# Attention values split into high and low parts at eviction, stored by head, with read-backs of outputs issued ahead of the last store

## Chip, core and metric

The kernel runs on one NeuronCore of a Trainium2 chip. The metric is the device time of one execution in microseconds (us). The core has a matrix engine (TensorE, PE in the profile, with PEld for its weight loads), VectorE (DVE), ScalarE (ACT), GpSimd (POOL), and SyncE (SP), whose queue issues most DMAs; ACT has a DMA queue too. All DMAs run on the same 16 DMA engines.

## What is computed

One layer of a transformer encoder for 1024 positions of 1024 features, all in float32: an adaLN modulation computed from `c`, two attention branches side by side, a gated merge, and a ConvFFN. Cut to what matters here:

```python
h = rmsnorm(x, g_mix) * (1 + scale1) + shift1
qa, ka, va, qb, kb, vb, ga, gb = split(h @ w_in)     # 8 heads of 64 columns in each branch
oa = mixture_of_dilations(qa, ka, va, rel_bias)      # windows (128,1), (512,4), (2048,16), merged per position
ob = neighbourhood_attention_2d(qb, kb, vb, na_rpb)  # 16 x 64 grid, 8 rows x 16 columns around each query
merged = sigmoid(ga) * (oa @ w_branch_dil) + sigmoid(gb) * (ob @ w_branch_na)
x = x + gate1 * (merged @ w_out)
h2 = rmsnorm(x, g_ffn) * (1 + scale2) + shift2
u_val, u_gate = split(depthwise_conv_seq(h2 @ w_up))
x = x + gate2 * ((gelu(u_gate) * u_val) @ w_down)
return rmsnorm(x, g_final)
```

## The kernel before, in words

**Precision.** A float32 operand is split into a rounded high part and a remainder, both of a type that TensorE multiplies at full rate (`FR`). A product is then three matmuls, high by high, high by low, low by high. The split is one ACT copy (`hi`) and one subtraction (`lo`) on DVE or POOL.

**Order of work.** Inside `tc.manual_schedule` (line 524 and 1356 to 1359) each engine executes its instructions in the order in which the program writes them; outside, a planner orders them. A tile of a pool with `bufs=n` reuses its buffer after n others, and the engine that writes it anew waits for its last reader, a DMA included.

**Projection (about 50 to 142 us).** `v_product`, `v_parts` and `v_wide` compute the values of both branches. A block is 128 positions (`st`, 0 to 7). Branch A's blocks 0 to 3 come in two halves of 256 columns; blocks 4 to 7 and all eight of branch B in one tile of 512 columns (`v_wide`). The order is `v_steps` (line 651): A's blocks 4 and 5 together in the two banks `pj` of `ps_g`, then 6 and 7 in the three banks `pv` of `ps_s`, then a step `None`, then B's blocks 0 to 7 in `pv`. Step `None` splits B's value weights (`v_split`: ACT the high parts, DVE and POOL the low ones), multiplies Q and K of the second position half in the two `pj` banks (lines 733 to 738), and starts POOL on sums for the next stage (`t_sums`) and on `a_operands`, which has one DVE subtraction (line 460) behind POOL's work.

In each step the program writes the matmuls, then `row_pairs` (a few multiply-adds of DVE over tiles of `w_ada`, 512 KB each, which SP loads seven ahead as their buffers come free, line 675), then `v_out` for the tiles of the step. `v_out` (line 313) copies the tile out of PSUM on ACT into one of two buffers `vs` and stores it: on SP's queue for the halves of blocks 0 to 3 and the last two blocks, on ACT's queue for the others. Values go to `va_s` or `vb_c` with one row of 512 columns per position.

**Rearranging in DRAM.** Keys' values are needed in chunks. `va_chunks` (line 412, six DMAs in step `None`) and `vb_chunks` (line 419, four calls of four DMAs in slots 54, 56, 59 and 61) copy the values from DRAM to DRAM into the order in which the heads read them.

**Heads (about 285 to 637 us).** Work is placed by hand in slots 0 to 101 (`at(slot, phase, job)`). A slot emits its jobs, phase by phase, and between them steps of `fill_steps`, matmuls of the gate columns of `w_in` that keep PE busy. `DilHead` (eight heads, one every 8 slots) and `NaHead` (eight heads, one every 4 slots from slot 64) load queries and keys, biases and values, multiply scores, apply softmax, turn the probabilities and multiply them by the values. `aside` queues ACT and DVE jobs to be emitted between fill steps, and `ensure(mark)` emits up to a mark.

The values of a head are loaded as float32 into the second half of a tile `vv` (`v_raw`, two buffers), three slots ahead of a `DilHead` (four DMAs) and two slots behind the start of a `NaHead` (four DMAs). `v_tile` (line 775) then splits them: ACT copies the high part to the first half, POOL subtracts in place.

`DilPair` merges the near and far outputs of two heads by shares: `send`, `load` of shares into two buffers `fb`, `weigh` on POOL in slots s0 + 27, 28, 30 and 31, `merge` in s0 + 32. Outputs go to `o_scr` in DRAM. `later(n, job)` puts a store n slots on; past the last slot it issues it at once.

**Hand-over (about 640 to 680 us).** Outputs are read back (`o_split`: a load into one of six buffers `oraw`, an ACT copy, a DVE subtraction), the gates are loaded (`gate_load`) and the branch weights `w_br` are loaded and split, all in `openers`, one at a fill step, while the last fill steps run. Then the branch products start.

Of the kernel before, what the change touches and what calls it, by code (L numbers as in the profile page):

```python
# [29 lines left out]
def hybrid_encoder(tc, xT, c, w_ada, small, w_in, p1_bias, p23_bias, na_bias, ln2_mult, ident, w_br, w_out,  # L30
# [8 lines left out]
    def f(ap):  # L39
        return ap.bitcast(FT)  # L40
# [239 lines left out]
    vb_c = dram.tile([S, 512], FT, name="vbc")  # L280
# [4 lines left out]
    v_scr = dram.tile([S + 9 * 128, 512], FT, name="v")  # L285
    va_s, va_b = v_scr[:S], v_scr[S:].rearrange("(j p) n -> j p n", j=9)
    vb_s = [v_scr[64 * sum(NA_NC[:cb]):64 * sum(NA_NC[:cb + 1])] for cb in range(4)]
# [24 lines left out]

    def v_out(br, st, p, c0=0, queue=sp):
        vs = work.tile([128, 512], FT, name="vs", bufs=2)[:, :p.shape[-1]]
        act.activation(vs, p, AF.Copy)
        queue.dma_start((va_s, vb_c)[br][st * 128:st * 128 + 128, c0:c0 + p.shape[-1]], vs)
# [94 lines left out]

    def va_chunks(cc):
        v4 = va_s.rearrange("(r t) n -> r t n", r=4)[:, :, cc]
        for r in range(4):
            sp.dma_start(va_b[1:8, 32 * r:32 * r + 32, cc], v4[r, 16:240].rearrange("(j p) n -> j p n", p=32))
        for j, t0 in ((0, 0), (8, 240)):
            sp.dma_start(va_b[j, 0:64, cc].rearrange("(r p) n -> r p n", r=4), v4[:, t0:t0 + 16])

    def vb_chunks(cb):
        t0, n = NA_T0[cb], NA_NC[cb]  # L420
        for r in range(4):
            sp.dma_start(vb_s[cb].rearrange("(w t r) n -> r w t n", r=4, t=n)[r],
                         vb_c[256 * r:256 * r + 256].rearrange("(w t) n -> w t n", t=16)[:, t0:t0 + n])
# [100 lines left out]
    with tc.manual_schedule(engines={e.engine for e in (sp, act, dve, pool, pe)}):  # L524
# [152 lines left out]
        def va_load(head, vr):  # L677
            cc = slice(64 * head, 64 * head + 64)
            sp.dma_start(vr[:, 0:8], va_s.rearrange("(t p) n -> p t n", p=128)[:, :, cc])
            sp.dma_start(vr[:, 8:15], va_b[1:8].rearrange("j p n -> p j n")[:, :, cc])  # L680
            for x_, j in ((0, 0), (64, 8)):
                sp.dma_start(vr[x_:x_ + 64, 15], va_b[j, 0:64, cc])

        def v_raw(load, head):
            vv = sm_pool.tile([128, 16, 128], FR, name="vv", bufs=2)
            load(head, f(vv[:, :, 64:128]))
            return vv
# [99 lines left out]
    for br, st in v_steps[10:]:  # L787
        v_out(br, st, *v_wide(st))
# [1310 lines left out]
```

## Time and profile before

| | |
|---|---|
| median of 3 runs | 1504.47 us (1503.78 to 1504.56) |
| profiled execution | 1502.23 us, of it the span of the instructions 1500.1 us |
| mean granted TensorE clock | 0.992 |
| TensorE busy | 97% of the span |
| DMA traffic | 241.13 MB, mean 161 GB/s |

The profile is of one execution. Its page gives busy times, the span in slices, the DMA queues, the chain of work that ended last, and the costliest groups. Answers of the trace show more: windows (busy time of each engine in a stretch, granted clock, share of the DMA engines in use), waits (who waited for whom), and the timeline (start, duration, engine, line, operation, what it writes and reads; in brackets the idle time ahead of it and what ended that). A row with "q" behind the engine's name (SPq, ACTq) is the issue of a DMA, not its transfer. Where an instruction waited for several things, the one that came last by the profile is named, which can be wrong where that engine had been done for long.

### The profile page before, as it was taken

Reading aid. Unit: us, or ns where it says so; the run is one execution under the profiler, and the core shown is the slowest. Engines: PE = TensorE matmul, PEld = TensorE weight load, DVE = VectorE, ACT = ScalarE, POOL = GpSimd, SP = SyncE. Lnnn points to the kernel's source line nnn. Section 1 sums busy time; section 2 is a strip of 40 time slices with the busy share of each in tenths; the row PEclk is TensorE's granted clock in tenths of the full one; section 3 lists DMA queues with packets and bytes.
Section 4 is the critical chain, followed back from the end, with each engine's and each line's share of the span. In section 5 each row is a group of like instructions: output and inputs, shape, how many; then the busy total and the mean of one; then the engine's idle time right before and its main releaser. Section 6 shows DMA issues by size and latency. Waiting matters only on the chain.

```text
span 1500.1 us, 21296 instructions
## 1 busy us (share of the span) xinstructions
PE 1451.6 (97%) x7308; PEld 1223.7 (82%) x7308; DVE 950.5 (63%) x1793; ACT 793.9 (53%) x1479; POOL 859.2 (57%) x706
## 2 busy tenths in 40 slices
PE   9999999999999879979999999999999999999998
PEld 8887888888888768857888778888888888887788
DVE  7696543356555646637625898666666667787865
ACT  6635543477776657644335555444444447574542
POOL 4156675434562555402257858766666676988712
PEclk9999999999999989999999999999999999999999
DMA  9586355866678999368744413222222234532313
GB/s 369 204 346 208 105 192 201 220 160 148 169 194 242 240 246 258 91 232 273 233 133 153 134 43 110 91 83 80 85 72 85 85 134 144 197 128 83 100 46 113
DMA packets 130515, 241.13 MB, mean 161 GB/s; under 512 B 47812, under 2 KB 60740, under 8 KB 130372
## 3 DMA queue, kind: packets, MB, share of 16 engines
q1 hardware_dynamic: 121752, 220.04, 47.7%
q10 hardware_dynamic: 8656, 19.73, 3.5%
q8 instruction: 58, 0.95, 0.3%
q14 instruction: 49, 0.40, 0.1%
HBM read 185.60 MB, written 59.90 MB: 164 GB/s over the span
## 4 chain that ended last, share of the span: by engine, by line
PE 41%; DVE 7%; DMA 4%; ACT 2%; issue 1%; POOL 1%; SPq 1%; DVEq 0%; ACTq 0%; POOLq 0%
PE pj L495 10%; PE pj L496 10%; PE pj L497 10%; PE pj L86 3%; PE pj L84 3%; PE pj L85 3%; DMA wraw<-w_down 1%; DVE op L1629 1%; DMA oraw<-w_ada 1%; DMA oraw<-oa 1%; DVE op L1548 1%; DMA big<-as 1%; DVE big L460 1%; ACT op L1547 1%; DVE x L1598 1%
## 5 line engine op out<-in xcount | busy, mean ns | idle before, releaser
L61 POOL TENSOR_TENSOR wlo<-wraw,whi 128x512 fp32r<-128x512 f32 (+1 forms) x90 | 113.9, 1287 | 140.9 <-ACT whi L57 139.1
L495 PE MATMUL pj<-op,wsh 128*128 128x512 f32 x408 | 158.5, 390 | 2.2 <-ACT wsh L57 2.2
L496 PE MATMUL pj<-op,wsh 128*128 128x512 f32 x408 | 158.7, 389 | 0.4 <-DVE op L1518 0.4
L497 PE MATMUL pj<-op,wsl 128*128 128x512 f32 x408 | 157.4, 389 | 0.0
L61 POOL TENSOR_TENSOR wsl<-big,wsh 128x512 fp32r<-128x512 f32 (+1 forms) x86 | 111.8, 1322 | 45.3 <-ACT wsh L57 40.4
L84 PE MATMUL pj<-h,whi 128*128 128x512 f32 x272 | 117.3, 431 | 3.5 <-ACT gs L1309 3.5
L85 PE MATMUL pj<-h,whi 128*128 128x512 f32 x272 | 108.3, 398 | 0.0
L86 PE MATMUL pj<-h,wlo 128*128 128x512 f32 x272 | 108.1, 398 | 0.0
L1728 DVE SCALAR_TENSOR_TENSOR big<-pj,sm,big 128x512 f32<-128x512 f32 (+2 forms) x183 | 94.9, 563 | 16.5 <-ACT big L1722 15.6
L875 DVE CUSTOM_DVE_ANT_0 P<-S,bias 128x256 f32<-128x256 f32 x128 | 49.1, 421 | 69.9 <-PE S L1015 40.5
L495 PEld LDWEIGHTS pj<-op,wsh 128*128 128x128 f32 x408 | 76.6, 188 | 18.9 <-ACT wsh L57 3.1
L495 PE MATMUL pj<-op,whi 128*128 128x512 f32 x232 | 90.7, 391 | 0.3 <-ACT wc L501 0.3
L496 PE MATMUL pj<-op,whi 128*128 128x512 f32 x232 | 90.5, 390 | 0.2 <-DVE op L1548 0.2
L497 PE MATMUL pj<-op,wlo 128*128 128x512 f32 x232 | 90.3, 389 | 0.0
L496 PEld LDWEIGHTS pj<-op,wsh 128*128 128x128 f32 x408 | 76.6, 188 | 16.8 <-DVE op L1518 0.9
L61 POOL TENSOR_TENSOR wsl<-wraw,wsh 128x384 fp32r<-128x384 f32 (+1 forms) x46 | 56.7, 1252 | 57.6 <-ACT wsh L57 50.0
L497 PEld LDWEIGHTS pj<-op,wsl 128*128 128x128 f32 x408 | 76.6, 188 | 16.0 <-POOL wsl L61 0.2
L876 ACT ACTIVATE P<-P,st 128x256 f32<-128x256 f32 x128 | 64.1, 502 | 38.3 <-DVE st L875 38.0
L889 DVE TENSOR_TENSOR tl<-T,th 128x512 fp32r<-128x512 f32 (+3 forms) x120 | 76.0, 648 | 5.2 <-ACT th L885 5.2
L57 ACT ACTIVATE whi<-wraw 128x1024 fp32r<-128x1024 f32 (+2 forms) x48 | 47.4, 992 | 57.7 <-PE pj L85 30.0
L1722 ACT ACTIVATE big<-pj,sm 128x512 f32<-128x512 f32 x61 | 47.0, 773 | 54.6 <-DVE pj L516 32.2
L516 DVE TENSOR_TENSOR pj<-pj,wc 128x512 f32<-128x512 f32 x40 | 27.8, 696 | 73.3 <-PE pj L497 73.3
(476 smaller groups left out, 4566.5 us busy)
## 6 DMA issues: line engine op xcount, KB each, us to landing
wada<-w_ada SPq DMA_DIRECT2D x31, 512.0 KB
qks<-qs ACTq DMA_DIRECT2D x28, 512.0 KB
wraw<-w_in SPq DMA_DIRECT2D x24, 512.0 KB
big<-w_up SPq DMA_DIRECT2D x22, 512.0 KB
wraw<-w_up SPq DMA_DIRECT2D x22, 512.0 KB
big<-as SPq DMA_DIRECT2D x22, 512.0 KB
as<-big SPq DMA_DIRECT2D x21, 512.0 KB
qs<-qks SPq DMA_DIRECT2D x32, 256.0 KB
```

What stands on the lines that cost most here:

```text
L57: act.activation(hi, raw, AF.Copy)
L61: lo_eng.tensor_tensor(lo[:, i:i + step], raw[:, i:i + step], f(hi)[:, i:i + step], OP.subtract)
L84: pe.matmul(psum, whi[:, k0 + k], mhi, start=k == 0, stop=False)
L85: pe.matmul(psum, whi[:, k0 + k], mlo, start=False, stop=False)
L86: pe.matmul(psum, wlo[:, k0 + k], mhi, start=False, stop=k == n - 1)
L495: pe.matmul(psum, whi[:, k], bhi, start=j < 4 and k == 0, stop=False, skip_group_check=True)
L496: pe.matmul(psum, whi[:, k], blo, start=False, stop=False, skip_group_check=True)
L497: pe.matmul(psum, wlo[:, k], bhi, start=False, stop=k == n - 1, skip_group_check=True)
L875: dve.tensor_tensor_reduce(pp, d, bias, -1.0, BIG, OP.add, OP.min, mi)
L876: act.activation(pp, pp, AF.Exp, bias=mi, scale=-1.0, accum_out=li)
L889: dve.tensor_tensor(tt[1][:m, :n], pt[:m, :n], f(tt[0])[:m, :n], OP.subtract)
L1728: dve.scalar_tensor_tensor(y[:, dst], src, wt, y[:, dst], OP.mult, OP.add)
```

## The change

The values are split as they leave PSUM. `v_out` works in pieces of 256 columns, four heads: ACT copies the high part, DVE subtracts it from the bank, and the tile `vs` holds high and low part of each head side by side, 128 columns. A store goes into a list, and `v_store(1)` issues all but the newest; one `v_store()` at the end issues what is left. In DRAM a head has 128 columns of each position, `va_s` and `vb_s` being of shape (1024, 8, 128), B's rows in the order of the grid.

`va_chunks` and `vb_chunks` and the tensors they filled are gone, as are `v_tile`'s split and its marks. Heads load the split values straight into `vv`, with the chunk order in the DMAs: `va_far` (one DMA) two slots ahead of a `DilHead`, `va_near` (six DMAs) at its start, `vb_load` for one of four column blocks at a time (four DMAs each) in slots s0 + 2 to s0 + 5 of a `NaHead`.

Smaller parts: `weigh` and `merge` of a pair each move by one slot; the last `NaHead` pair's output has a buffer of its own in `gspool`; gate stores of the last slot and behind it are issued by ACT; `w_br[0]` is loaded in the fill step n = 14; `later` collects what falls past the last slot in `tail`, whose stores are issued behind the first six read-backs (`o_load`); the openers start three fill steps later.

```diff
+    va_s, vb_s = (dram.tile([S, 8, 128], FT, name=n) for n in ("va", "vb"))
...
+    v_stores = []
+
+    def v_store(keep=0):
+        while len(v_stores) > keep:
+            queue, dst, src = v_stores.pop(0)
+            queue.dma_start(dst, src)
+
     def v_out(br, st, p, c0=0, queue=sp):
-        vs = work.tile([128, 512], FT, name="vs", bufs=2)[:, :p.shape[-1]]
-        act.activation(vs, p, AF.Copy)
-        queue.dma_start((va_s, vb_c)[br][st * 128:st * 128 + 128, c0:c0 + p.shape[-1]], vs)
+        rows = vb_s.rearrange("(v p r) n c -> r v p n c", v=2, r=4)[st // 2, st % 2] if br else \
+            va_s[st * 128:st * 128 + 128]
+        for n0 in range(0, p.shape[-1] // 64, 4):
+            vs = work.tile([128, 4, 128], FR, name="vs", bufs=2)
+            src = p[:, 64 * n0:64 * n0 + 256].rearrange("p (n c) -> p n c", c=64)
+            act.activation(vs[:, :, 0:64], src, AF.Copy)
+            dve.tensor_tensor(vs[:, :, 64:128], src, f(vs)[:, :, 0:64], OP.subtract)
+            v_stores.append((queue, rows[:, c0 // 64 + n0:c0 // 64 + n0 + 4], f(vs)))
+            v_store(1)
...
-                va_chunks(slice(0, 512))
...
+        def va_far(head, vr):
+            sp.dma_start(vr[:, 0:8], va_s[:, head].rearrange("(t p) c -> p t c", p=128))
+
+        def va_near(head, vr):
+            v4 = va_s[:, head].rearrange("(r t) c -> r t c", r=4)
+            for r in range(4):
+                sp.dma_start(vr[32 * r:32 * r + 32, 8:15], v4[r, 16:240].rearrange("(j p) c -> p j c", p=32))
+            for x_, t0 in ((0, 0), (64, 240)):
+                sp.dma_start(vr[x_:x_ + 64, 15], v4[:, t0:t0 + 16])
...
+    def vb_load(head, vr, cb):
+        v4 = vb_s[:, head].rearrange("(g w x) c -> w x g c", g=4, w=4)
+        t0, n = 4 * NA_T0[cb], 4 * NA_NC[cb]
+        for w in range(4):
+            sp.dma_start(vr[n * w:n * w + n, 4 * cb:4 * cb + 4], v4[w, t0:t0 + n])
...
-    def v_tile(vv, parts):
-
-        lo = vv[:, :, 64:128]
-        for m, cs_ in parts:
-            act.activation(vv[:m, cs_, 0:64], f(lo[:m, cs_]), AF.Copy)
-            pool.tensor_tensor(lo[:m, cs_], f(lo[:m, cs_]), f(vv[:m, cs_, 0:64]), OP.subtract)
...
     def later(n, job):
         if now[0] + n > LAST:
-            job()
+            tail.append(job)
...
-                at(s0 - 3, "first", self.load_v)
+                at(s0 - 2, "first", self.load_v)
+                at(s0, "first", lambda: va_near(self.head, f(self.vv)))
...
-            for n, g, z in ((27, 1, 0), (28, 1, 1), (30, 0, 0), (31, 0, 1)):
+            for n, g, z in ((28, 1, 0), (29, 1, 1), (31, 0, 0), (32, 0, 1)):
...
-            at(s0 + 4, "last", self.prepare)
...
+                at(s0 + 2 + n, "first", lambda cb=cb: vb_load(self.head, f(self.vv), cb))
...
-            later(1, lambda: sp.dma_start(g_scr[n][:, halves[hf]], g))
+            if now[0] < LAST:
+                later(1, lambda: sp.dma_start(g_scr[n][:, halves[hf]], g))
+            else:
+                act.dma_start(g_scr[n][:, halves[hf]], g)
...
+            elif n == 14:
+                w_raw[0] = w_load(w_br[0])
...
-    for n, cb in zip((54, 56, 59, 61), (0, 3, 1, 2)):
-        at(n, "first", vb_chunks, cb)
...
+    for job, *args in openers[:4] + openers[5:7]:
+        o_load(*args)
+    for job in tail:
+        job()
     for n in range(21):
...
-        if openers:
+        if openers and n > 2:
             opener(*openers.pop(0))
```

More of the change, by code (lines that the diff above doesn't have):

```diff
@@ L675, in row_pairs, with v_tile @@
                     rows[n + 7] = pair_load(*pairs[n + 7])
[L677 to L687, printed above, removed]
+        def va_far(head, vr):
[6 more added lines that the diff above has]
+                sp.dma_start(vr[x_:x_ + 64, 15], v4[:, t0:t0 + 16])
+        def v_tile():
+            return sm_pool.tile([128, 16, 128], FR, name="vv", bufs=2)
         def dil_bias(head):
@@ L788, in hybrid_encoder @@
         v_out(br, st, *v_wide(st))
+    v_store()
     work.release()
@@ L973, in __init__ @@
             self.P, self.tt, self.po = {}, {}, {}
+            at(s0, "first", self.begin)
             if self.head > 1:
@@ L994, in load_v, with begin @@
         def load_v(self):
-            values[self.head] = v_raw(va_load, self.head)
+            values[self.head] = v_tile()
+            va_far(self.head, f(values[self.head]))
+        def begin(self):
+            self.bt, self.vv = biases.pop(self.head), values.pop(self.head)
         def prepare(self):
@@ L999, in prepare @@
             pool.tensor_tensor(bt[:, 512:896], bt[:, 512:896], lnm, OP.add)
-        def values(self):
-            self.bt, self.vv = biases.pop(self.head), values.pop(self.head)
-            for n in range(0, 16, 8):
-                self.mark = aside(600, lambda n=n: v_tile(self.vv, ((128, slice(n, n + 8)),)))
         def far_scores(self, r):
@@ L1114, in __init__ @@
                 at(s0 + 26, "first", self.load, 1, z)
-            for n, g, z in ((27, 1, 0), (28, 1, 1), (30, 0, 0), (31, 0, 1)):
+            for n, g, z in ((28, 1, 0), (29, 1, 1), (31, 0, 0), (32, 0, 1)):
                 at(s0 + n, "last", self.weigh, g, z)
-            at(s0 + 32, "first", self.merge)
+            at(s0 + 33, "first", self.merge)
         def begin(self):
@@ L1216, in load @@
             if self.i == 0:
-                oTs[self.head // 2] = at_pool.tile([128, S], FT, name=("u1", "u23")[self.head // 2 % 2])
-            self.vv = v_raw(vb_load, self.head)
-        def prepare(self):
-            for part in ((96, slice(0, 4)), (128, slice(4, 12)), (96, slice(12, 16))):
-                self.mark = aside(500, lambda part=part: v_tile(self.vv, (part,)))
+                oTs[self.head // 2] = (gspool.tile([128, S], FT, name="last", bufs=1) if self.head == 6 else
+                                       at_pool.tile([128, S], FT, name=("u1", "u23")[self.head // 2 % 2]))
+            self.vv = v_tile()
         def bias(self, cb):
@@ L1389, in gate_load, with o_load @@
         sp.dma_start(gates[i], g2[i // 2][:, :, halves[i % 2]])
+    o_raw = {}
+    def o_load(br, pr, hf):
+        raw = o_raw[br, pr, hf] = opool.tile([128, 512], FT, name="oraw", bufs=6)
+        sp.dma_start(raw, o_scr[br][pr][:, halves[hf]])
     def o_split(br, pr, hf):
         hi, lo = (t[:, pr, halves[hf]] for t in o[br])
-        raw = opool.tile([128, 512], FT, name="oraw", bufs=6)
-        sp.dma_start(raw, o_scr[br][pr][:, halves[hf]])
+        if (br, pr, hf) not in o_raw:
+            o_load(br, pr, hf)
+        raw = o_raw.pop((br, pr, hf))
         act.activation(hi, raw, AF.Copy)
```

34 lines of the change are left out of this document (6 added, 28 removed).

## The prediction

> **What bounds the kernel now.** I read the page first, then the windows by stage, then who TensorE waited for.
>
> ```profile
> span 1500.1 us, 21296 instructions
> PE 1451.6 (97%) x7308; PEld 1223.7 (82%) x7308; DVE 950.5 (63%) x1793; ACT 793.9 (53%) x1479; POOL 859.2 (57%) x706
> 50.00:142.00 92.00, 91.70 (x458) 76.62 (x459) 73.25 (x98) 38.89 (x69) 41.08 (x25) 1.00 0.68 251
> 142.00:285.00 143.00, 142.18 (x628) 117.09 (x627) 61.44 (x90) 59.95 (x92) 82.74 (x65) 1.00 0.49 164
> 285.00:480.00 195.00, 191.96 (x1222) 170.13 (x1220) 111.14 (x380) 147.67 (x405) 94.57 (x88) 1.00 0.72 184
> 480.00:640.00 160.00, 140.22 (x863) 124.03 (x862) 95.75 (x293) 99.07 (x264) 85.90 (x76) 0.95 0.78 209
> 640.00:680.00 40.00, 31.64 (x126) 23.75 (x125) 16.43 (x23) 18.18 (x26) 5.49 (x4) 0.96 0.77 257
> ```
>
> The columns are the stage, its length, busy time of PE, PEld, DVE, ACT and POOL with instruction counts, granted clock, DMA share and GB/s. TensorE is the bound: idle time elsewhere is worth nothing unless it reaches PE. The stages that the change touches are projection (50 to 142), dilated heads (285 to 480), neighbourhood heads (480 to 640) and the hand-over (640 to 680). PE has idle time to win only in the last three: 3.0, 19.8 and 8.4 us. In the projection it idles 0.3 us in 92, so there it can only lose. Who made PE wait, and what a wait does to its clock:
>
> ```profile
> PE T L1271 <- POOL P L1262: 9.0, 2, 6.0
> PE T L1125 <- DVE tl L889: 5.4, 1, 5.4
> PE pj L84 <- ACT gs L1309: 3.5, 1, 3.5
> 490.00:492.00 2.00, 1.24 (x4) 0.50 0.98 197
> 492.00:494.00 2.00, 2.00 (x8) 0.50 1.04 248
> 494.00:496.00 2.00, 2.00 (x10) 0.61 1.02 246
> 489.16 0.46 DVE L1252 CUSTOM_DVE_ANT_0 P<-S,bias 128x288 f32<-128x288 f32 x1 [7.50 <-DMA bias<-na_bias]
> 536.99 1.26 POOL L1179 TENSOR_TENSOR u<-u,fb 128x512 f32<-128x512 f32 x1 [8.19 <-DMA fb<-fcs]
> ```
>
> The engines named were late because of DMAs: DVE stood 7.50 us for a bias, POOL 8.19 us for merge weights. The stall of 5.4 us ended at 490.8, and the three window rows (length, PE busy, granted clock) show the clock at 0.50 to 0.61 for the five us behind it: a stall of this size costs 2.5 us on top of itself. Over the whole stage the mean of 0.95 on 140 busy us makes 0.05 x 140 = 7 us. Waits and clock are 19.8 + 7 = 27 us in the neighbourhood stage and 8.4 + 0.04 x 32 = 9.7 us in the hand-over. That is all that can be won.
>
> **The change, part by part.**
>
> *Values split on leaving PSUM.* Each eviction of 256 columns becomes one ScalarE copy, one VectorE subtract that reads the same bank, and a 256 KB store. There are 32 such pieces (8 tiles of 256, 12 of 512) for 20 evictions.
>
> ```profile
> L315 ACT ACTIVATE vs<-pv x18: 366/574/600, 51.4 to 142.4; 128x512 f32<-128x512 f32 x10, 128x256 f32<-128x256 f32 x8
> 475.51 0.69 DVE L889 TENSOR_TENSOR tl<-T,th 128x512 fp32r<-128x512 f32 x1
> 478.04 0.55 DVE L889 TENSOR_TENSOR tl<-T,th 128x384 fp32r<-128x384 f32 x1
> ```
>
> ACT: 12 x (2 x 0.37 - 0.60) = +1.7 us. DVE: 0.69 at 512 and 0.55 at 384 columns give an estimate of 0.41 at 256, so 32 x 0.41 = 13 us on an engine already busy 73 of 92. What decides is the order. There are two buffers `vs`, and `v_store(1)` keeps one store back: the store of piece n is issued only behind the copy of piece n + 1, and the copy of piece n + 2 needs its buffer. So ACT, in the hand-written order, stands a whole store latency L between issuing a store and the next copy; VectorE's subtracts, its w_ada sums and the bank's release queue behind that. L, from issue to the buffer being free, is bounded by these rows:
>
> ```profile
> 51.74 24.43 SPq L316 DMA_DIRECT2D v<-vs  x8
> 53.90 0.82 ACT L315 ACTIVATE vs<-pv 128x256 f32<-128x256 f32 x2 [1.91 <-DMA v<-vs]
> 77.80 0.34 ACTq L316 DMA_DIRECT2D v<-vs  x1
> 85.85 0.60 ACT L315 ACTIVATE vs<-pv 128x512 f32<-128x512 f32 x1 [7.00 <-PE pv L310]
> 78.58 13.91 SPq L145 DMA_DIRECT2D wada<-w_ada  x10
> ```
>
> Quiet: 53.90 - 51.74 = 2.2 us (128 KB, two copies later). Beside the w_ada loads: 85.85 - 77.80 = 8.05 us. The releaser named there is PE, but the block in question was done five us earlier, so I read this wait as the store of two evictions before. The Trainium skill (DMA: Bandwidth & Descriptors, Anatomy of one DMA) fits 2.0 us plus bytes over 436 GB/s for another issue path, which gives an estimate of 2.6 us for 256 KB; the loaded row is three times that, and by the page the delay worked out below would lie near its lower end.
>
> Now the chain, in blocks of 128 positions. These rows give the pace before:
>
> ```profile
> 73.85 0.75 DVE L669 TENSOR_SCALAR pcol<-wada,cs 128x512 f32<-128x512 f32 x1
> 80.16 0.71 DVE L181 STREAM_TRANSPOSE mt<-sq 128x512 f32<-128x512 f32 x1
> 80.91 0.69 DVE L185 TENSOR_REDUCE mt<-mt 128x16 f32<-128x512 f32 x1
> 85.61 0.39 PE L84 MATMUL pj<-h,whi 128*128 128x512 f32 x1
> 88.75 1.15 ACT L57 ACTIVATE vwh<-wraw 128x512 fp32r<-128x512 f32 x2 [0.40 <-ACT vs L315]
> 90.04 1.30 POOL L61 TENSOR_TENSOR vwl<-wraw,vwh 128x512 fp32r<-128x512 f32 x1 [38.10 <-ACT vwh L57]
> 96.49 0.39 PE L308 MATMUL pv<-vwh,h 128*128 128x512 f32 x1
> 122.06 3.01 POOL L61 TENSOR_TENSOR kl<-ks,kl 128x512 fp32r<-128x512 f32 x2
> 122.14 1.76 DVE L460 TENSOR_TENSOR wraw<-wraw,ks 128x512 f32<-128x512 f32 x1 [6.94 <-POOL wlo L61]
> 122.69 0.60 ACT L315 ACTIVATE vs<-pv 128x512 f32<-128x512 f32 x1 [3.23 <-DMA vbc<-vs]
> 140.37 0.39 PE L310 MATMUL pv<-vwh,h 128*128 128x512 f32 x1
> ```
>
> One w_ada pair is (80.16 - 73.85) / 4 = 1.58 us of DVE, a fold 0.71 + 0.69 = 1.4. First with L = 2.2, its least:
>
> - Second column half of blocks 0 to 3: a subtract, a store, a copy, two subtracts and the reduce ahead of the sums, 0.4 + 2.2 + 0.4 + 0.8 + 0.4 from 73.6, so the sums start at 78, not 73.85, and their first four pairs end at 84.3.
> - Block 3's store stands on SP behind the loads that these four pairs set free: issued at 84.3, landed at 86.5. Blocks 4 and 5 have three copies (0.4) and two stores left: 86.5 + 1.2 + 4.4 = 92.1, with the subtract 92.5. Only then is the second bank of `pj` free for the Q/K product that PE begins at 85.6: **a stall of 7 us**.
> - Blocks 6 and 7 each cost DVE three pairs (4.7) and two subtracts (0.9), the first also a fold: 92.5 + 7.0 + 5.6 = 105.1. Behind block 7's copies on ACT stands the split of the next value weights: at 104.8 instead of 88.75, **S = 16 us**. PE, through the Q/K product 10.9 us after 92.5, waits for it again.
> - POOL does its part of that split from 90.04 and then one chain without a gap to 125, on which DVE's L460 waits at 122.14. All of it moves by S. Then DVE still owes 1.76, a fold, two pairs (3.1) and two subtracts (0.9) before block 2's bank is free: 129.3 + S. Before, ACT alone freed it at 122.69 + 0.6 = 123.3, and PE wanted it at 123.8 (blocks of 5.5 us from 96.49). So PE loses 5.5 + S there, and the remaining blocks keep it: **21.5 us, and 2.5 of clock behind the stall, 24 at least.**
>
> With the loaded row for block 3's store it lands at 84.3 + 8.05 = 92.4 and the bank is free at 98.4. With L = 4, half of that row, for blocks 6 and 7, a block's two pieces take two stores, two copies and an issue, 2 L + 1.1 = 9.1, and the weight split starts at 98.4 + 7.0 + 9.1 - 0.5 = 114: S = 25. Late in the stage that period is 3.6 above PE's 5.5, some 12 us over the last blocks, if L stays. I take S = 20, between the two, and 3 us for the late blocks: 20 + 5.5 + 2.5 + 3 = **+31**, bounds +24 and 25 + 5.5 + 2.5 + 12 = +45. From 142 to 285 PE is busy 142.2 of 143, so nothing gives it back.
>
> *Values in the heads.* Gone: forty ACT copies and forty POOL subtracts. PE's own work hid them; only the 3.0 idle us of the dilated stage could hang on them: -0.5, bounds 0 and -3. Its loads (far ones at two slots before a head, near ones, six DMAs for three, at the head's start, needed eight slots on) are covered by those slots. Gone too: the DRAM-to-DRAM copies.
>
> ```profile
> L422 SPq DMA_DIRECT2D v<-vbc x16: 520/592/597, 454.3 to 479.9; - x16
> L780 POOL TENSOR_TENSOR vv<-vv x40: 720/1288/1312, 288.5 to 629.7; 128x512 fp32r<-128x512 f32 x24, 96x256 fp32r<-96x256 f32 x16
> q1 hardware_dynamic: 2114, 0.52, 42.6%
> 582.09 1.96 SPq L773 DMA_DIRECT2D vv<-v  x4
> ```
>
> Those sixteen copies (28 x 64 rows of 2 KB, 3.7 MB) end just before the late bias; without the last four the bias is issued 4 x 0.59 = 2.4 us sooner and finds less queued, so the first stall and its clock (5.4 + 2.5) should mostly go. Weighing one slot later covers part of the POOL wait. Against it: rows of 512 bytes for 256. The window from 318 to 324 us, nearly all such a load, costs 0.426 x 16 x 6 us / 2114 = 19 ns of one engine a packet; 1792 packets a head at one to two times that are 0 to 2.2 us more on sixteen engines. The Trainium skill (DMA: Bandwidth & Descriptors, Specifications) puts full rate at 512 bytes and more, by which it would be near 0. And 16 loads a head for 4: 12 x 0.49 = 5.9 us more of SP, where a head has 160 / 8 = 20 us and the same queue issues queries, keys, biases, merge weights and gate stores; behind a late value load stand the next head's biases, and PE's output matmul now waits for it directly. I take -10, the first stall and a little, bounds -22 (most of the 27) and +8 (the SP time of one and a half heads reaching PE).
>
> *Hand-over.* `w_br[0]` is loaded during the fill, the last gate stores go by ACT, and six read-backs precede the last pair's store.
>
> ```profile
> 621.17 14.70 SPq L1310 DMA_DIRECT2D gs<-gs  x2
> 645.19 0.63 ACT L1395 ACTIVATE o0hi<-oraw 128x512 fp32r<-128x512 f32 x1 [6.78 <-DMA oraw<-oa]
> ```
>
> SP stood 14.7 us in these two stores, and ACT then 6.78 us for the first read-back, with PE behind it. On SP the load of `w_br[0]` (0.4 us) moves ahead of the last heads' loads, and six read-backs (2.7 us at 0.45) ahead of the last pair's store, so that pair is read back some 3 us later; the gate stores cost ACT 0.33 us each, and the openers start three fill steps later, 2 us that the fill's matmuls cover. Most of the 9.7 goes: -6, bounds 0 and -9.7. Next late is the last pair's read-back.
>
> **Sum.** Profiled execution 1502.2 us (span 1500.1 and 2.1 around it): +31 - 0.5 - 10 - 6 = +14.5, 1516.7. The median of the runs shown, 1504.5, lies 2.2 above this execution; the forecast for such a median is **1519**.
>
> **Rivals.** (1) *The evictions stay covered* (faster). If a store lands in about 2.2 us and the banks come free before PE needs them, the projection loses nothing and the gains remain: -16.5, 1488. It decides at 2 L + 1.1 = 5.5, so L = 2.2. The quiet row speaks for it; the 8.05 us row, and that even 2.2 left PE waiting for banks, speak against. (2) *SP becomes the bound of the neighbourhood stage*: +8 there in place of -10, 1537. For it 5.9 us a head; against, much SP time there was itself waiting. (3) *Gains and loss cancel*: least loss 24 against 17 + 8 won: 1503.5. For it, all stalls there had DMAs behind them; against, the heads' loads grow.
>
> **Chances.** Forecast 0.55, (1) 0.17, (2) 0.15, (3) 0.13. The forecast's own bounds are 1504.5 + 24 - 25 - 3 = 1500 and 1504.5 + 45 + 8 = 1557 where all go one way; the range 1490 to 1543 holds nearly all of it, (2) and (3), and the slower half of (1). A measurement of this kernel tells about 0.2%, 3 us, from no change: faster 0.21 ((1) and a part of (3)), same 0.07, slower 0.72.
>
> **What would show it.** Right: PE waits of several us near 86 to 97, near 105 to 117 and before the sixth `vb` block, ACT's copies into `vs` waiting for stores, a projection that ends 24 us or more after 142; no 5.4 us wait at the first neighbourhood bias; no 6.78 us wait of ACT at the read-back. Wrong: a projection as long as before, which would mean that the copies do not wait or the banks are free earlier; or SP never idle from 495 to 640.

## The result, and the profile after

The changed kernel took **1546.68 us** (median of 4 runs, 1545.03 to 1551.2), the kernel before beside it 1504.51 (4 runs, 1503.78 to 1505.57): ratio 1.0284, 95% interval 1.0261 to 1.0308, or 42 us slower. The profiled execution took 1545.03 us, its span is 1543.3.

First the page of the changed kernel, then its windows by stage (stage, length, busy time of PE, PEld, DVE, ACT and POOL, granted clock, DMA share, GB/s).

```profile
span 1543.3 us, 21431 instructions
PE 1461.9 (95%) x7308; PEld 1230.1 (80%) x7308; DVE 958.9 (62%) x1825; ACT 779.8 (51%) x1451; POOL 818.0 (53%) x666
```

```profile
50.00:142.00 92.00, 73.31 (x341) 59.33 (x340) 60.55 (x90) 27.11 (x54) 26.77 (x14) 0.87 0.60 205
142.00:185.00 43.00, 34.26 (x136) 26.26 (x135) 26.17 (x44) 17.96 (x34) 20.11 (x16) 0.89 0.40 142
525.00:685.00 160.00, 126.04 (x772) 110.70 (x771) 87.64 (x279) 85.00 (x228) 62.66 (x51) 0.98 0.85 221
685.00:725.00 40.00, 39.41 (x205) 33.35 (x205) 21.29 (x34) 22.11 (x37) 7.57 (x6) 1.00 0.73 245
```

TensorE has the same 7308 matmuls. In the projection it was busy 91.7 of 92 us; now 73.3 of the first 92 and 34.3 of the next 43, at a clock of 0.87 to 0.89. The neighbourhood stage has 34 idle us in 160 where it had 19.8. Only the hand-over is better: 39.4 busy of 40, where it was 31.6.

The stages move, so windows at fixed times don't compare them. Points that both programs have do: the first matmul of the values and the last, the first turn of a dilated head and the last, the first score of a neighbourhood head and the last output, the first matmul of `w_out`.

| from, to | before | after | difference |
|---|---|---|---|
| projection: first to last matmul of values | 63.8 to 140.4 | 64.7 to 176.3 | +35.9 at its end |
| to the first turn of a dilated head | 288.1 | 328.9 | +4.9 |
| to the last turn of a dilated head | 473.2 | 517.8 | +3.8 |
| to the first neighbourhood score | 483.1 | 527.7 | 0.0 |
| to the last neighbourhood output | 637.4 | 696.0 | +14.0 |
| to the first matmul of `w_out` | 752.6 | 799.5 | -11.7 |
| to the end of the span | 1500.1 | 1543.3 | -3.7 |

The last row is the same code. Over the profiles of this study it lasts 743.8 to 747.5 us, so a difference of 3 or 4 us in one profile says nothing.

**Projection.** The largest waits of PE from 45 to 185 us (who waited for whom, total us, times, longest), and the timeline of ACT:

```profile
PE pj L84 <- DVE vs L324: 9.5, 2, 6.8
PE pv L305 <- ACT vwh L57: 7.2, 1, 7.2
PE pv L305 <- DVE vs L324: 6.9, 3, 4.3
```

```profile
80.78 0.38 ACT L323 ACTIVATE vs<-pj 128x256 fp32r<-128x256 f32 x1 [2.29 <-DMA va<-vs]
92.69 0.39 ACT L323 ACTIVATE vs<-pj 128x256 fp32r<-128x256 f32 x1 [11.53 <-DMA va<-vs]
...
94.95 0.34 ACTq L315 DMA_DIRECT2D va<-vs  x1
97.04 0.39 ACT L323 ACTIVATE vs<-pj 128x256 fp32r<-128x256 f32 x1 [1.79 <-DMA va<-vs]
...
104.21 0.33 ACTq L315 DMA_DIRECT2D va<-vs  x1
109.96 0.38 ACT L323 ACTIVATE vs<-pv 128x256 fp32r<-128x256 f32 x1 [5.37 <-DMA va<-vs]
...
115.75 0.38 ACT L323 ACTIVATE vs<-pv 128x256 fp32r<-128x256 f32 x1 [5.41 <-DMA va<-vs]
...
116.21 1.15 ACT L57 ACTIVATE vwh<-wraw 128x512 fp32r<-128x512 f32 x2
```

Of ACT's 21 copies into `vs` from 76 to 175 us, 15 wait for a store (`va<-vs`, `vb<-vs`), five for VectorE's subtract and one for PE. The longest wait, 11.53 us, ends at 92.69: that is the store of block 3, which SP issued at 85.89 behind four `w_ada` loads. From a store's issue to the copy that needs its buffer it is 97.04 - 94.95 = 2.1 us where nothing else loads (DMA share 0.34), 109.96 - 104.21 = 5.75 beside the `w_ada` loads (0.93). The split of the next value weights starts at 116.21 instead of 88.75.

**Neighbourhood heads.** Waits of PE (520 to 690) and of DVE (525 to 690), the wait of DVE before the change (483 to 640), then SP's timeline (start, length, line, what it loads, how many):

```profile
PE T L1261 <- DVE tl L881: 20.9, 11, 4.9
PE T L1261 <- DVE stb L1249: 13.2, 11, 3.4
```

```profile
DVE P L1242 <- DMA bias<-na_bias: 49.9, 14, 8.2
```

```profile
DVE P L1252 <- DMA bias<-na_bias: 9.9, 2, 7.5
```

```profile
618.63 0.58 SPq L65 DMA_DIRECT2D wraw<-w_in  x1
619.25 8.22 SPq L770 DMA_DIRECT2D vv<-vb  x8
627.58 0.36 SPq L1220 DMA_DIRECT2D bias<-na_bias  x1
```

PE waits for DVE, and DVE for a bias, 14 times and 49.9 us, where it was twice and 9.9 before. The bias comes late: eight value loads hold SP for 8.22 us ahead of it. (A row of several issues runs from the first to the last and takes in SP's waits between them.) Counted issue by issue, SP issues for 102.7 of the 155 us from 535 to 690; before, for 75.3 of the 140 from 490 to 630.

### The profile page after: what moved, and what is told of

It reads as the page before. It is cut to its first block, busy times and chain, and to the rows that moved or that the text cites. A ratio compares the mean times of both kernels' runs of the same rounds, so it can differ in the third digit from the quotient of the medians.

```text
span 1543.3 us, 21431 instructions
## 1 busy us (share of the span) xinstructions
PE 1461.9 (95%) x7308; PEld 1230.1 (80%) x7308; DVE 958.9 (62%) x1825; ACT 779.8 (51%) x1451; POOL 818.0 (53%) x666
## 4 chain that ended last, share of the span: by engine, by line
PE 67%; DMA 14%; DVE 8%; ACT 3%; issue 3%; SPq 3%; POOL 2%; ACTq 0%; DVEq 0%; POOLq 0%
PE pj L492 13%; PE pj L494 13%; PE pj L493 13%; PE pj L84 6%; PE pj L86 6%; PE pj L85 6%; DMA bias<-na_bias 2%; DMA vb<-vs 2%; DMA gs<-gs 2%; DMA kl<-qks 2%; DMA va<-vs 2%; DMA oraw<-w_ada 1%; PE T L1024 1%; PE O L1088 1%; SPq L770 1%
## 5 line engine op out<-in xcount | busy, mean ns | idle before, releaser
L1730 DVE SCALAR_TENSOR_TENSOR big<-pj,sm,big 128x512 f32<-128x512 f32 (+2 forms) x183 | 94.9, 562 | 16.5 <-ACT big L1724 15.6
L493 PEld LDWEIGHTS pj<-op,wsh 128*128 128x128 f32 x408 | 76.6, 188 | 16.7 <-DVE op L1520 0.9
L492 PEld LDWEIGHTS pj<-op,wsh 128*128 128x128 f32 x408 | 76.6, 188 | 16.5 <-ACT wsh L57 0.6
L494 PEld LDWEIGHTS pj<-op,wsl 128*128 128x128 f32 x408 | 76.6, 188 | 16.0 <-POOL wsl L61 0.2
L61 POOL TENSOR_TENSOR wsl<-wraw,wsh 128x384 fp32r<-128x384 f32 (+1 forms) x46 | 57.0, 1260 | 57.6 <-ACT wsh L57 49.9
L1252 POOL TENSOR_SCALAR P<-P,stb 128x288 f32<-128x288 f32 (+1 forms) x32 | 39.3, 1229 | 86.2 <-DVE stb L1249 33.7
```

The costliest lines, as they stand in the source:

```text
L61: lo_eng.tensor_tensor(lo[:, i:i + step], raw[:, i:i + step], f(hi)[:, i:i + step], OP.subtract)
L492: pe.matmul(psum, whi[:, k], bhi, start=j < 4 and k == 0, stop=False, skip_group_check=True)
L493: pe.matmul(psum, whi[:, k], blo, start=False, stop=False, skip_group_check=True)
L494: pe.matmul(psum, wlo[:, k], bhi, start=False, stop=k == n - 1, skip_group_check=True)
L1730: dve.scalar_tensor_tensor(y[:, dst], src, wt, y[:, dst], OP.mult, OP.add)
```

## The experiments

Stage lengths below are measured as in the table: projection from the first matmul of values to the last (76.6 before, 111.6 after), neighbourhood stage from the first score to the last output (154.3 before, 168.3 after). Four profiles with the changed kernel's code in the neighbourhood stage gave 163.3 to 168.7 us, so a stage length in one profile is known to some 5 us.

### Projection: stores or VectorE's order

**Stores left out, first try.**

```diff
-            queue.dma_start(dst, src)
+            pass
...
```

> After, with the stores of the value pieces left out (the heads read x in place of the values, copied behind the projection). In before the last value block ended at 140.6 us, in after at 176.6, 36 us later. Theory (ACT waits for one store between two copies, two buffers): only the subtractions and their order on VectorE stay, about 8 to 10 us by the same chain with no store in it (the weight split 2.5 us late, block 2's bank behind L460), so the last value block ends near 149 to 152. Rival (VectorE's subtractions and the order of its sums alone hold the PSUM banks): it still ends near 170 or later.

One run: 1536.59 us, projection 92.2. Eight plain copies from `x` fill `va_s` and `vb_s` in place of the stores. They were issued at 39 to 45 us, ahead of the stage instead of behind it, and held its first matmul back from 64.7 to 79.1 us, so the time doesn't tell the theories apart. The run was made again with the copies later.

**Stores left out, copies later.** The same edit, with the eight copies in SP's own order behind the loads for the last `w_ada` sums.

> The changed kernel with the value stores of the projection left out (the stores' bytes are written to the same tensors from x by eight plain copies on SP behind the whole projection, so the heads read wrong values but the same number of bytes). The evictions themselves, ACT's copy and VectorE's subtract of each piece, stay. In the changed kernel the projection lasts 111.6 us (64.7 to 176.3), before 76.6. If the wait of ACT for a kept-back store is the main part of the 36 us lost there, the projection should end near 150 to 157 and the time fall by 17 to 25 us to some 1522 to 1530. Rival, VectorE's order alone (subtracts behind w_ada sums, the next subtract ahead of the bank) loses it: the projection ends at 170 or later and the time stays above 1538. The earlier run without stores gave a length of 92.2 us, but its copies ran at the start of the stage and held it back; if that distorted nothing else, 64.7 + 92 = 157.

One run: 1527.73 us, and a projection that ends at 156.0, both inside the first theory's bands. The copies were issued at 121.5 to 127.3 us, while the last value blocks still ran and not behind the projection. The row of the value matmuls (first and last start behind the durations), changed kernel and this one, and the start of the weight split in this one:

```profile
L307 PE MATMUL pv<-vwh,h x80: 387/389/628, 76.3 to 176.3; 128*128 128x512 f32 x80
```

```profile
L307 PE MATMUL pv<-vwh,h x80: 387/389/629, 75.6 to 156.0; 128*128 128x512 f32 x80
97.68 1.14 ACT L57 ACTIVATE vwh<-wraw 128x512 fp32r<-128x512 f32 x2
```

Without stores the stage still ends 15.6 us later than before the change. So of 35.9 us, 20.3 hang on the stores, and 15.6 on the order of the copies and subtracts alone. The weight split starts 97.68 - 88.75 = 8.9 us late without stores, 27.5 with them. PE's largest wait there:

```profile
PE pv L305 <- DVE vs L324: 6.5, 1, 6.5
```

VectorE frees the bank late, behind its `w_ada` sums. Neither cause alone makes the loss; the theory that named the stores as the main part holds for somewhat more than half.

**A third buffer.** Every third piece goes to a buffer of its own (the last two blocks keep two buffers), and the second-half stores of blocks 0 to 3 go by ACT's queue:

```diff
+    vs_homes = itertools.cycle([(work, "vs", 2), (work, "vs", 2), (early, "vs3", 1)])
...
-            vs = work.tile([128, 4, 128], FR, name="vs", bufs=2)
+            home, name, bufs = next(vs_homes)
+            vs = home.tile([128, 4, 128], FR, name=name, bufs=bufs)
...
-            v_out(0, st, pvs[1][st], 256)
+            v_out(0, st, pvs[1][st], 256, queue=act)
...
+    vs_homes = itertools.cycle([(work, "vs", 2)])
```

> The changed kernel with every third piece of the projection in a third buffer vs3, and the second-half stores of blocks 0 to 3 issued on ACT's queue instead of SP's. If ACT's copies wait for the store of two pieces before, a third buffer gives each store a whole piece more: the 11.5 us wait at 92.7 should go, the weight split should start near 98 to 106 instead of 116.2, the projection end near 155 to 165 instead of 176.3, and the time fall by 10 to 20 us to some 1527 to 1537. Rival, VectorE's order decides: the waits move from stores to VectorE, the end stays within 4 us of 176 and the time within 4 us of 1546.7.

Measured: 1528.62 us (4 runs, 1524.73 to 1530.4), ratio to the kernel before 1.0176 (1.0156 to 1.0196): by the ratios 16 us better than the change as made, by the medians 18. The projection ends at 163.1. All three lie in the first theory's bands. ACT's timeline in this kernel:

```profile
97.52 0.38 ACT L325 ACTIVATE vs<-pv 128x256 fp32r<-128x256 f32 x1 [6.25 <-DVE vs L326]
...
104.07 0.39 ACT L325 ACTIVATE vs<-pv 128x256 fp32r<-128x256 f32 x1 [5.68 <-DMA va<-vs]
104.53 1.15 ACT L57 ACTIVATE vwh<-wraw 128x512 fp32r<-128x512 f32 x2
```

The 11.5 us wait is gone, and the weight split starts 11.7 us earlier, at 104.53: 15.8 behind the kernel before. What is left are waits for VectorE and stores by turns. The buffer and the other queue came together, so this run doesn't part them. The projection gives 13 us of the gain; the neighbourhood stage, whose code is the same, was 163.3 in this profile for 168.3.

### Hand-over

The part of the change at the hand-over (early `w_br[0]`, last gate stores by ACT, a buffer of its own for the last pair, six read-backs ahead of the last pair's store) on the kernel before:

```diff
+            elif n == 14:
+                w_raw[0] = w_load(w_br[0])
...
+            if now[0] < LAST:
+                later(1, lambda: sp.dma_start(g_scr[n][:, halves[hf]], g))
+            else:
+                act.dma_start(g_scr[n][:, halves[hf]], g)
...
+    for job, *args in openers[:4] + openers[5:7]:
+        o_load(*args)
+    for job in tail:
+        job()
```

> Before with the hand-over part of the change alone: six read-backs ahead of the last pair's store, gate stores at the end on ACT, the first branch weights loaded earlier, openers three fill steps later. Theory (in after the stretch from the last output matmul to the first w_out matmul was 11.7 us shorter, so this part earns it by itself): 6 to 12 us faster than before, 1493 to 1498. Rival (it was shorter only because loads had time to come early while PE stood in the neighbourhood stage): within 3 us of before.

Measured: 1488.76 us, ratio 0.9928 (0.9904 to 0.9952), 11 to 12 us faster: the theory's size. From the last output to the first matmul of `w_out` it is 102.6 us instead of 115.2. Windows of this kernel over the hand-over:

```profile
637.00:656.00 19.00, 19.00 (x90) 15.91 (x90) 10.79 (x15) 12.74 (x21) 2.99 (x2) 1.00 0.83 275
656.00:680.00 24.00, 24.00 (x108) 19.87 (x107) 16.42 (x25) 12.38 (x16) 5.49 (x5) 1.00 0.88 283
```

PE has no idle time left here, and a full clock. This part of the change is worth 11 to 12 us by itself.

### Neighbourhood heads: issues, bytes, order

**More issues on the kernel before.** Each of a head's four value loads is cut in four; bytes and rows stay:

```diff
-            sp.dma_start(vr[:16 * n, 4 * cb:4 * cb + 4], vb_s[cb].rearrange("(g p) n -> p g n", g=4)[:, :, cc])
+            src = vb_s[cb].rearrange("(g p) n -> p g n", g=4)[:, :, cc]
+            for w in range(4):
+                sp.dma_start(vr[4 * n * w:4 * n * w + 4 * n, 4 * cb:4 * cb + 4], src[4 * n * w:4 * n * w + 4 * n])
```

> Before, with each of the four value loads of a neighbourhood head cut into four DMAs; bytes and rows unchanged, 12 issues a head more on SP. Theory (issues on SP): 8 to 15 us slower than before, with DVE waiting for biases. Rival (bytes): within 2 us of before.

Measured: 1525.37 us, ratio 1.0154 (1.0129 to 1.018); the stage 175.9 us for 154.3. The direction is that of the issue theory, the size, 23 to 24 us, twice its forecast.

**Issues on ACT's queue.** In the changed kernel ACT issues the sixteen loads:

```diff
-            sp.dma_start(vr[n * w:n * w + n, 4 * cb:4 * cb + 4], v4[w, t0:t0 + n])
+            act.dma_start(vr[n * w:n * w + n, 4 * cb:4 * cb + 4], v4[w, t0:t0 + n])
```

> After, with the 16 value loads of each neighbourhood head issued by ACT's queue in place of SP's; bytes and rows unchanged. From the first neighbourhood scores to the last output matmul before took 154 us, after 168 us. Theory (SP has no time left: biases stand in its queue behind value loads): that stretch falls to 155 us or less and the whole by 10 us or more against after, about 1535. Rival (the DMA engines are full with rows of 512 bytes): the stretch stays within 3 us of 168. Second rival (ACT then stands in the issues and takes SP's place): 165 or more.

Measured: 1562.89 us, ratio 1.0411 (1.0377 to 1.0445), the stage 183.2: slower, as the second rival had it. It moves the wait: VectorE no longer waits for biases but for ACT, which stands in its issues. The two largest waits of DVE there:

```profile
DVE u L1286 <- ACT u L1282: 23.7, 9, 4.1
DVE tl L881 <- ACT th L877: 21.1, 13, 4.7
```

**Four loads a head in the changed kernel.** The same bytes in rows of the same size, in another order of positions:

```diff
-        for w in range(4):
-            sp.dma_start(vr[n * w:n * w + n, 4 * cb:4 * cb + 4], v4[w, t0:t0 + n])
+        sp.dma_start(vr[:4 * n, 4 * cb:4 * cb + 4],
+                     vb_s[:, head].rearrange("(g p) c -> p g c", g=4)[4 * t0:4 * t0 + 4 * n] if 4 * (t0 + n) <= 256 else
...
```

> The changed kernel with one load for each column block of a neighbourhood head, 4 a head for 16, of the same bytes in rows of the same 512 bytes; it reads positions in another order, so those heads weigh wrong values. If SP's time for issues is what lengthened the neighbourhood stage (168.3 us from the first score to the last output, before 154.3), it falls to 145 to 156 and the time by 12 to 22 us, to 1525 to 1535. If it is the bytes and rows on the DMA engines, it stays within 3 us of 168 and the time within 4 us of 1546.7.

Measured: 1538.95 us (1536.31 to 1540.96), ratio 1.0242 (1.0223 to 1.0262); the stage 163.4. A gain of 6 by the ratios and 8 by the medians, less than the 12 to 22 of the issue theory and more than the rival's 4: a miss for both. SP now issues for 56 of the 148 us from 532 to 680, and still DVE waits 26.5 us for biases. Something else was close behind the issues; the last table of this part shows what.

**The kernel before with its first stall taken away.** To have a base without the stall at the first neighbourhood bias, the hand-over part was kept and the copies of branch B's values moved:

```diff
-    for n, cb in zip((54, 56, 59, 61), (0, 3, 1, 2)):
+    for n, cb in zip((3, 5, 9, 11), (0, 3, 1, 2)):
```

So early, the copies overwrite rows of branch A's values that later heads still read. A second run gives them a tensor of their own:

```diff
-    vb_s = [v_scr[64 * sum(NA_NC[:cb]):64 * sum(NA_NC[:cb + 1])] for cb in range(4)]
+    vbs = dram.tile([64 * sum(NA_NC), 512], FT, name="vbs")
+    vb_s = [vbs[64 * sum(NA_NC[:cb]):64 * sum(NA_NC[:cb + 1])] for cb in range(4)]
```

> The kernel before with two things alone: the hand-over part of the change (w_br early, last gate stores by ACT, read-backs ahead of the last pair's store, a buffer of its own for the last pair), and the sixteen DRAM copies of branch B's values moved from slots 54 to 61 to slots 3 to 11. The hand-over part alone gave 1488.8, ratio 0.993. If the copies just ahead of the neighbourhood heads delayed the bias on which PE waited 5.4 us and lost 2.5 us of clock, moving them gives another 4 to 8 us: 1481 to 1485. If the bias is late for other reasons, the stall at 490 stays and the time is within 3 us of 1488.8. If the copies now delay the first dilated heads, that stage gets longer and the time is above 1490.

> As the run with the hand-over part and the sixteen DRAM copies of branch B's values moved to slots 3 to 11 (1480.1 us), but the copies have a tensor of their own: in that run they shared rows with branch A's values, which later heads still read, and overwrote part of them. The same time is expected, 1478 to 1483, and the neighbourhood stage at 143 to 147 us (144.7 there, 154.3 before). Rival: another place in DRAM costs bandwidth; then the first neighbourhood stall returns and the time is nearer to 1489.

Measured: 1480.06 us, and with a tensor of its own 1479.73 (5 runs, 1477.1 to 1484.03), ratio 0.9833 (0.9807 to 0.986), as the theory had it or a little better. The stage is 143.9 us, 10.4 shorter than before (with the hand-over part alone it was 155.2); DVE's waits for biases there come to

```profile
DVE P L1255 <- DMA bias<-na_bias: 2.4, 1, 2.4
```

So the copies just ahead of the heads did make the first bias late. This kernel beats both others, and it is the right base to price the loads: the changed kernel has no such copies either, and its stage is 168.3 - 143.9 = 24.4 us longer than this one's.

**Bytes, issues and both on that base.** Doubled bytes: each load of seven of the eight heads takes along the 64 columns of the head before.

```diff
-        cc = slice(64 * head, 64 * head + 64)
+        cc = slice(64 * head - (64 if head else 0), 64 * head + 64)
...
-            self.vv = v_raw(vb_load, self.head)
+            self.vv = sm_pool.tile([128, 16, 128], FR, name="vv", bufs=2)
+            vb_load(self.head, f(self.vv) if self.head else f(self.vv[:, :, 64:128]))
```

The issues are cut in four as in the first experiment of this part.

> The kernel of the run before it in this batch with the bytes of seven of the eight neighbourhood heads' value loads doubled and nothing else: each load takes the 64 columns of the head before along, so rows of 512 bytes for 256, in the same four loads; the split then writes over the extra half. The changed kernel moves the same bytes there. If it is the doubled bytes that lengthen the changed kernel's neighbourhood stage (168.3 us, and still 163.4 with four loads a head, against 144.7 with the early copies), the stage here grows from 145 to 155 to 163 and the time by 10 to 18 us, to 1490 to 1498. If it is the number of issues and the order on SP, the stage stays within 3 us of 145 and the time within 4 us of the run before it.

> The best kernel so far (hand-over part, early DRAM copies; 1479.7 us, neighbourhood stage 143.9) with sixteen value loads a neighbourhood head for four, the same bytes and rows. On the kernel before, twelve more issues a head made the stage 21.6 us longer, but with the stall at its start in both. If issues alone cost that much, the stage is 160 to 168 here and the time 1496 to 1504. Rival: issues cost mostly where the stage already starts late; then the stage grows by the 5 us that the changed kernel lost on them, to 147 to 152, and the time to 1483 to 1489.

> The same with both: doubled bytes (rows of 512 bytes, seven of eight heads) and sixteen value loads a head. The changed kernel's stage is 163 to 169 us in its profiles, 24 above the best kernel's. If bytes and issues are the whole account, this stage is 163 to 170 and the time 1498 to 1506, whether the two add (10 + 22 would give 176) or overlap. If something else of the change makes a third of it (placing in four slots, the step between rows, the missing split), this stage stays at 154 to 160 and the time at 1488 to 1496.

| on the best kernel | time | ratio to the kernel before | stage | DVE for biases |
|---|---|---|---|---|
| as it is | 1479.73 | 0.9833 (0.9807 to 0.986) | 143.9 | 2.4 |
| doubled bytes | 1488.36 | 0.989 (0.9862 to 0.9919) | 154.1 | 16.0 |
| sixteen issues for four | 1506.51 | 1.0014 (0.9997 to 1.0031) | 172.5 | 42.5 |
| both | 1507.57 | 1.0027 (1.0012 to 1.0042) | 168.7 | 35.3 |

SP's timeline, with sixteen issues and with four:

```profile
531.18 11.31 SPq L776 DMA_DIRECT2D vv<-vbs  x16
542.60 1.30 SPq L1235 DMA_DIRECT2D bias<-na_bias  x3
...
553.57 9.36 SPq L776 DMA_DIRECT2D vv<-vbs  x16
563.03 0.83 SPq L1235 DMA_DIRECT2D bias<-na_bias  x2
```

```profile
542.48 3.93 SPq L774 DMA_DIRECT2D vv<-vbs  x4
546.50 1.26 SPq L1233 DMA_DIRECT2D bias<-na_bias  x2
```

The issues alone lengthen the stage by 28.6 us and bring back its long waits for biases; bytes alone cost 10.2; both together cost no more than the issues, 24.8, which is what the changed kernel lost (24.4). The medians say the same: 26.8, 8.6 and 27.8 us. Against the bands, the issues cost more than forecast (160 to 168), the bytes came out just below theirs (155 to 163) and clear of the rival's, and both together fell inside (163 to 170), 1.6 us above in time. A load cut in four is also a smaller load, and no run parts the two.

From a head's first value load to its last, SP needs 10.4 us with sixteen and 3.0 with four, on the mean of the eight heads: 7.4 more, of which 28.6 / 8 = 3.6 reach TensorE. Of the 10.4 only 6.3 is issuing. What SP waits for between the issues, in the changed kernel from 525 to 690:

```profile
SPq L770 <- DMA kl<-qks: 8.3, 10, 2.0
SPq L770 <- DMA qs<-qks: 6.0, 9, 0.8
SPq L770 <- DMA ks<-qks: 5.8, 8, 0.8
```

The value loads (L770) wait until queries and keys have landed, which they neither read nor write. Each of the 239 DMAs that SP issues in this kernel's neighbourhood stage reuses the semaphore (the counter that tells of a landing) of the one that SP issued eight before, and waits until that one has landed. So a load costs SP its issue and, where eight are under way, a wait for a landing. Summed over the single issues of the stage, in us:

| kernel | stage | issues | issuing | waiting for a landing | waiting for an engine |
|---|---|---|---|---|---|
| before | 154.3 | 146 | 80.0 | 17.8 | 51.5 |
| best kernel | 143.9 | 142 | 77.8 | 14.0 | 46.6 |
| best, doubled bytes | 154.1 | 142 | 75.6 | 33.4 | 41.4 |
| best, sixteen issues | 172.5 | 238 | 105.0 | 37.5 | 20.2 |
| best, both | 168.7 | 238 | 103.7 | 35.2 | 19.7 |
| changed | 168.3 | 239 | 106.3 | 36.4 | 16.0 |
| changed, four loads | 163.4 | 145 | 60.4 | 74.0 | 27.3 |

Sixteen loads add 27.2 us of issuing and 23.5 of landings, and SP's waits for engines, its slack, shrink by 26.4; the 24.3 that are left and some 4 us of short gaps are the 28.6 by which the stage grows. With both, the DMA engines were less in use (share 0.75 from 484 to 655) than with doubled bytes alone (0.89 from 484 to 640): where SP is the bound, the extra bytes find time. The changed kernel with four loads has little to issue and stands for landings instead; that is what was close behind the issues. No run changed the eight.

**Order and place in the changed kernel.** The value loads behind the next head's bias, and, with four loads a head, all four in one slot:

```diff
-                at(s0 + 2 + n, "first", lambda cb=cb: vb_load(self.head, f(self.vv), cb))
+                at(s0 + 2 + n, "last", lambda cb=cb: vb_load(self.head, f(self.vv), cb))
```

> The changed kernel with the four value loads of a slot issued at the slot's end, behind the next head's bias, instead of ahead of it. DVE waited for biases 49.9 us in the changed kernel. If the biases are late because they stand behind value loads on SP, the stage falls from 168.3 to 150 to 160 us and the time by 8 to 18 us, to 1529 to 1539. If it is the bytes on the DMA engines that make them late, the stage stays within 4 us of 168 (the bias then shares the engines with the same loads) and the time within 4 us of 1546.7.

```diff
-                at(s0 + 2 + n, "first", lambda cb=cb: vb_load(self.head, f(self.vv), cb))
+                at(s0 + 2, "first", lambda cb=cb: vb_load(self.head, f(self.vv), cb))
```

> The changed kernel with four value loads a neighbourhood head, as in the run with 4 for 16 (1539.0 us, stage 163.4; it reads positions in another order, so those heads weigh wrong values), and all four issued at one slot, s0 + 2, as before the change, instead of one at each of s0 + 2 to s0 + 5. Bytes, rows and issues are then those of the kernel with doubled bytes (stage 154.1). If it is the placing in four slots that makes up the 9 us between these two, the stage falls to 152 to 157 and the time to 1528 to 1534. If it is the place of the rows in DRAM (a step of 4 KB between rows for 2 KB) or the missing split on ACT and POOL, it stays at 160 to 166 and the time at 1535 to 1543.

The order alone does nothing: 1545.63 us, stage 168.0. So it is not that single loads stand ahead of a bias, but that SP as a whole runs late. One slot for four loads: 1537.14 us (1534.63 to 1538.75) for 1538.95, a time in the second band; the stage, 158.0 for 163.4, lies between the two. SP's waits for landings fall from 74.0 to 38.8 us, but the stages differ by about the 5 us to which one profile knows them, so whether placing counts, and what separates the 158.0 here from the 154.1 of the best kernel with doubled bytes, stays open.

## Why the prediction failed

The direction was right and the size wrong: +14.5 us forecast, +42 measured, above the range. Of the 28 us between them the neighbourhood term makes 24. (The forecast's lower bound of 1500 is not the sum of its terms' bounds, 24 - 3 - 22 - 9.7, which makes 1494; its upper one, 1557, is, and the range cut it off at 1543.) By its terms:

- **Projection, +31 (24 to 45): measured +35.9**, the mechanism as forecast. ACT stands for stores, PE waits at the Q/K product, behind the weight split and for `vb` banks. The delay S of the weight split was put at 20 between 16 and 25; it was 116.21 - 88.75 = 27.5. The store of block 3 landed at 92.69, by the loaded row (92.4 worked out); in part that is luck, since it was issued at 85.89 for 84.3 and took 6.8 us for 8.05. Blocks 6 and 7 had L = 5.75, where 4 was taken. With S = 27.5 the prediction's own sum makes 38.5 for the 35.9, so its other terms were together a little too large. The floor of 16 holds stores of 2.2 us: without any the split came 8.9 late, with the third buffer, where ACT still waited for stores, 15.8. The Trainium skill (DMA: Bandwidth & Descriptors, Anatomy of one DMA), by which the prediction had an estimate of 2.6 us for a store, lies near the quiet 2.1 and not near the 5.75 beside `w_ada` loads.
- **What follows the projection, 0: measured +4.9.** The prediction said that nothing there gives the loss back; it did not see that the stall has a tail. The window behind it, and the same stretch before:

```profile
176.30:210.00 33.70, 30.16 (x122) 23.50 (x122) 18.08 (x32) 22.59 (x44) 15.12 (x12) 0.95 0.19 71
```

```profile
140.40:174.00 33.60, 32.77 (x144) 26.42 (x143) 19.80 (x31) 24.23 (x42) 23.18 (x18) 1.00 0.19 62
```

  PE idles 3.5 us for 0.8, and 0.05 x 30.2 = 1.5 us of its busy time go to the clock: 4.2 of the 4.9.
- **Dilated heads, -0.5 (0 to -3): measured +3.8 in this profile**, and 0 to 2.9 in others with the same loads (185.1 with the third buffer, 185.8 and 187.1 with four loads, 186.3 with the other order, 188.0 without stores, where it was 185.1 before). Freeing ACT and POOL brought nothing that can be seen. That the added loads cost something was not tried by itself.
- **Neighbourhood heads, -10 (-22 to +8): measured +14. This step failed.** What it expected to win was there: with the copies out of the way the stage is 10.4 us shorter. What failed is "I take -10, the first stall and a little", which priced the loads at nearly nothing. The prediction had a price from rows, 5.9 us of SP a head for issuing (on the best kernel SP's run of loads got 7.4 longer, waits for landings included), and held against it that "much SP time there was itself waiting", allowing it at most for one and a half heads. SP did have waits for engines to give, 46.6 us in the stage of the best kernel, but only 26.4 of them were given up for the 50.7 that sixteen loads added in issuing and landings. The changed kernel's stage is 24.4 us longer than the best kernel's, about 3 a head, and sixteen loads alone are enough for it. The doubled bytes were put at 0 to 2.2 us a head on the DMA engines; alone they cost 10.2 / 8 = 1.3, with sixteen issues nothing on top. Order on SP was not it.
- **Hand-over, -6 (0 to -9.7): measured -11.7**, alone 12.6 of stage and 11 to 12 of time. All that was in sight went, where the prediction took two thirds. The kernel before, from its last output on:

```profile
637.00:656.00 19.00, 15.47 (x72) 12.57 (x72) 6.44 (x8) 5.76 (x10) 2.97 (x2) 1.00 0.62 198
656.00:680.00 24.00, 19.17 (x72) 13.78 (x71) 10.74 (x17) 13.07 (x18) 2.53 (x2) 0.93 0.80 272
```

  That is 3.5 + 4.8 us idle and 0.07 x 19.2 = 1.3 of clock, 9.6, the prediction's bound of 9.7. ACT's wait of 6.78 us at the first read-back is gone, none there is longer than 1.7. The other 2 us are within what the same code differs from profile to profile; no run accounts for them.

The sum 35.9 + 4.9 + 3.8 + 14.0 - 11.7 - 3.7 is 43.2, the difference of the spans. **Rival 2**, SP as the bound of the neighbourhood stage, is the one that came true, at 14 us for its 8; it had 0.15. SP issues or stands for a landing in 142.7 of the stage's 168.3 us. Its 1537 fell short by 10: the projection took 5 more, its tail 5, the dilated heads 4 and the neighbourhood stage 6, while the hand-over gave 6 more and the end of the span 4. Rival 1 fell with the projection; rival 3 fell with it too, and with the gain that the neighbourhood stage didn't bring.

## What to carry to other kernels

A queue that issues loads in order for many readers may have less slack than its waits suggest. Price added loads at what a run of them takes on that queue for every head, waits for landings included (7.4 us here, of which 3.6 reached TensorE), and look at who is queued behind. Work taken off engines that were hidden brings nothing, and what it costs elsewhere (a second reader of a PSUM bank, a store that a two-buffer ring waits for, twice the bytes) lands on the path. When a change has several parts, time them alone: here one part was worth some 12 us, the cause of a stall could be moved for another 9, and the main part lost more than twice both.

## What was not expected of the hardware

- A run of sixteen value loads kept SP for 10.4 us on the mean of eight heads, 0.65 a load, though the median issue took 0.37: the rest are mostly waits until a DMA issued eight before had landed.
- Doubling the bytes of value loads cost 10.2 us of stage with four issues a head and nothing with sixteen (168.7 against 172.5): the two limits overlap instead of adding.
- A 256 KB store took 2.1 us from issue to the copy that reuses its buffer where nothing else loaded, and 5.75 beside the `w_ada` loads.
